# Row softmax, aligned code on DVE and ACT: padding that is executed instead of a branch over it

## The chip, the cores and the metric

One core of one Trainium2 chip. The time is that of one execution on the device in microseconds (us), the median of several. A profile of one execution goes with each kernel; its span runs from the first to the last instruction and is about 2 us shorter than the time (315.6 us of 317.42 in the kernel before). Engines: DVE is VectorE, ACT is ScalarE, SP is SyncE, which here only issues loads; "DVEq", "ACTq" and "SPq" are their sequencers.

## The reference

```python
def setup_inputs():
    batch, seq, dim = 32, 512, 1024
    return {
        "x": np.random.randn(batch, seq, dim).astype(np.float32),
        "temperature": 0.5,
    }

def reference(x, temperature):
    scaled = x / temperature
    shifted = scaled - np.max(scaled, axis=-1, keepdims=True)
    exp_x = np.exp(shifted)
    return (exp_x / np.sum(exp_x, axis=-1, keepdims=True)).astype(np.float32)
```

64 MiB are read and 64 MiB are written, 134 MB in all.

## The kernel before

Sixteen tiles of 128 partitions with eight rows each (4 MiB) go through six buffers. SP issues the loads; DVE takes the maximum of four rows per partition at a time and later multiplies by the reciprocal of the sum; ACT computes the exponential with its sum and issues the stores. A new load is issued when the store of the tile six places earlier has given its buffer free.

```python
TILES = [[8]] * 16
BUFS = 6
GROUP = 4
# ... cut: pools, groups, DRAM access patterns
    def load():                                   # on SP
        i = len(tiles)
        if i < len(TILES):
            xt = data.tile([P, sum(TILES[i]), d], f32, name="xt")
            nc.sync.dma_start(out=xt, in_=dram(xf, i))
            tiles.append(xt)
    # ... cut: maximum (DVE), exponential (ACT), divide (DVE)
    def store(g):                                 # on ACT, then the next load
        i, _, _, part = groups[g]
        if part:
            a, k = part
            nc.scalar.dma_start(out=dram(of, i)[:, a : a + k, :], in_=tiles[i][:, a : a + k, :])
            if a + k == sum(TILES[i]):
                load()

    with tc.manual_schedule():

        nc.vector.addr_align(128, offset=0, max_nops=0)
        nc.scalar.addr_align(128, offset=0, max_nops=0)
        for _ in range(BUFS):
            load()
        for g in range(len(groups) + 1):
            if g < len(groups):
                maximum(g)
                exponential(g)
            if g > 0:
                divide(g - 1)
                store(g - 1)
```

`addr_align(128, offset=0)` makes the next instruction of that engine lie at a multiple of 128 instruction slots. The slots up to there hold padding, of which the kernel's text doesn't tell the number. With `max_nops=0` a branch jumps over it (one COMPARE_BRANCH on each engine in the trace of the kernel before, 47 ns on DVE and 33 ns on ACT); with the default it is executed as NOPs.

Of the kernel before, what the change touches and what calls it, by code (L numbers as in the profile page):

```python
# [1 line left out]

# [4 lines left out]
# [9 lines that stand above are left out]
@with_exitstack  # L16
def kernel(
    ctx: ExitStack,
    tc: tile.TileContext,
    x: bass.AP,  # L20
    temperature: bass.AP,
    out: bass.AP,
):
    nc = tc.nc
    f32 = mybir.dt.float32
    scale = 1.0 / float(temperature)
    extreme = mybir.AluOpType.max if scale > 0 else mybir.AluOpType.min

    P = 128
    xf = x.flatten_outer_dims()  # L30
    of = out.flatten_outer_dims()
    n, d = xf.shape
    assert sum(sum(ks) for ks in TILES) * P == n

    data = ctx.enter_context(tc.tile_pool(name="data", bufs=BUFS))
    stats = ctx.enter_context(tc.tile_pool(name="stats", bufs=4))


    groups, first, r = [], [], 0
    for i, ks in enumerate(TILES):  # L40
        first.append(r)
        r += sum(ks)
        a = 0
        for k in ks:
            for b in range(0, k, GROUP):
                m = min(GROUP, k - b)
                groups.append((i, a + b, m, (a, k) if b + m == k else None))
            a += k

    def dram(t, i):  # L50
        k = sum(TILES[i])
        block = t[P * first[i] : P * (first[i] + k), :]
        return block.rearrange("(p k) d -> p k d", p=P, k=k)

    tiles, small = [], []

    def load():
# [6 lines that stand above are left out]
    def maximum(g):  # L64
        i, a, k, _ = groups[g]
        top, bias, sums, recip = (
            stats.tile([P, k], f32, name=name) for name in ("top", "bias", "sums", "recip")
        )
        small.append((bias, sums, recip))
        nc.vector.tensor_reduce(  # L70
            out=top, in_=tiles[i][:, a : a + k, :], axis=mybir.AxisListType.X, op=extreme
        )
        nc.vector.tensor_scalar_mul(bias, in0=top, scalar1=-scale)  # L73

    def exponential(g):
        i, a, k, _ = groups[g]
        bias, sums, _ = small[g]
        for b in range(k):
            nc.scalar.activation(  # L79
                tiles[i][:, a + b, :],  # L80
                tiles[i][:, a + b, :],
                mybir.ActivationFunctionType.Exp,
                bias=bias[:, b : b + 1],
                scale=scale,
                accum_out=sums[:, b : b + 1],
            )

    def divide(g):
        i, a, k, _ = groups[g]
        _, sums, recip = small[g]  # L90
        nc.vector.reciprocal(recip, sums)  # L91
        for b in range(k):
            nc.vector.tensor_scalar_mul(  # L93
                tiles[i][:, a + b, :], in0=tiles[i][:, a + b, :], scalar1=recip[:, b : b + 1]
            )

    def store(g):
# [8 lines that stand above are left out]

    with tc.manual_schedule():

        nc.vector.addr_align(128, offset=0, max_nops=0)
        nc.scalar.addr_align(128, offset=0, max_nops=0)  # L110
        for _ in range(BUFS):
            load()
        for g in range(len(groups) + 1):
# [8 lines that stand above are left out]
# [1 line left out]
_INS = ['x', 'temperature']  # L123
_OUTS = [((32, 512, 1024), 'float32')]

_NUMBERS = {'temperature': 0.5}


# [26 lines left out]
```

## Time and profile before

| | before |
|---|---|
| median time, 3 runs ahead of the prediction | 317.71 us (317.61 to 318.15) |
| span of the profiled run | 315.6 us |
| DVE busy, ACT busy | 75%, 47% |
| share of the DMA engines' time in loads and stores | 49.7% + 49.2% |
| first reduction on DVE | 13.42 us |

The chain of waits of its first 20 us (columns: start in us, length in us, what; the work that ended last, followed backwards) says what the first reduction waits for:

```profile
0.67 0.07 issue
0.73 12.66 DMA xt<-in_x_dram
13.39 0.02 issue
13.42 4.43 DVE top L70
```

The chain runs through SP's issue of the first load at 0.73 us and the load itself. The branches of DVE and ACT, taken at 0.8 and 0.7 us, aren't in it.

### The profile page before, as it was taken

Reading aid. Unit: us, or ns where it says so; the run is one execution under the profiler, and the core shown is the slowest. Engines: PE = TensorE matmul, PEld = TensorE weight load, DVE = VectorE, ACT = ScalarE, POOL = GpSimd, SP = SyncE. Lnnn points to the kernel's source line nnn. Section 1 sums busy time; section 2 is a strip of 40 time slices with the busy share of each in tenths; the row PEclk is TensorE's granted clock in tenths of the full one; section 3 lists DMA queues with packets and bytes.
Section 4 is the critical chain, followed back from the end, with each engine's and each line's share of the span. In section 5 each row is a group of like instructions: output and inputs, shape, how many; then the busy total and the mean of one; then the engine's idle time right before and its main releaser. Section 6 shows DMA issues by size and latency. Waiting matters only on the chain.

```text
span 315.6 us, 622 instructions
## 1 busy us (share of the span) xinstructions
DVE 235.5 (75%) x224; ACT 149.6 (47%) x257; POOL 0.2 (0%) x4
## 2 busy tenths in 40 slices
DVE  0299999999789494994939949498594976949720
ACT  0176666666626255361553615546065560645500
POOL 0000000000000000000000000000000000000000
DMA  8999999999999999999999999999999999999996
GB/s 330 415 448 415 386 457 407 461 411 453 424 440 432 432 432 429 444 424 453 415 454 407 457 407 457 403 461 403 461 403 461 403 462 403 461 419 444 428 436 278
DMA packets 4613, 134.26 MB, mean 425 GB/s; under 512 B 512, under 2 KB 512, under 8 KB 512
## 3 DMA queue, kind: packets, MB, share of 16 engines
q1 hardware_dynamic: 2304, 67.11, 49.7%
q10 hardware_dynamic: 2304, 67.11, 49.2%
q14 instruction: 5, 0.04, 0.0%
HBM read 67.11 MB, written 67.11 MB: 425 GB/s over the span
## 4 chain that ended last, share of the span: by engine, by line
DVE 72%; another core or an unknown queue 15%; DMA 4%; ACT 3%; issue 1%; DVEq 0%
DVE top L70 43%; DVE xt L93 27%; DMA xt<-in_x_dram 4%; ACT xt L79 3%; DVE recip L91 1%; DVE bias L73 1%; DVEq L150 0%
## 5 line engine op out<-in xcount | busy, mean ns | idle before, releaser
L79 ACT ACTIVATE xt<-xt,bias 128x1024 f32<-128x1024 f32 x128 | 145.4, 1137 | 136.0 <-DVE recip L91 118.6
L70 DVE TENSOR_REDUCE top<-xt 128x4 f32<-128x4096 f32 x32 | 141.3, 4416 | 62.2 <-DMA xt<-in_x_dram 62.2
L93 DVE TENSOR_SCALAR xt<-xt,recip 128x1024 f32<-128x1024 f32 x128 | 87.7, 749 | 1.1
L79 ACT ACTIVATION_READ_ACCUMULATOR xt<-xt,bias 128x1 f32 x128 | 23.8, 186 | 0.0
L79 ACT ACT_TABLE_LOAD x1 | 1.3, 1283 | 13.5 <-DMA xt<-in_x_dram 13.5
L91 DVE RECIPROCAL recip<-sums 128x4 f32<-128x4 f32 x32 | 5.5, 171 | 2.1 <-ACT xt L79 2.1
L73 DVE TENSOR_SCALAR bias<-top 128x4 f32<-128x4 f32 x32 | 5.5, 170 | 1.1
L136 POOL MEMSET const-bfloat16-1.0<- 128x1 bf16 x1 | 0.1, 102 | 0.0
L136 POOL MEMSET const-uint8-127<- 128x1 uint8 x1 | 0.1, 102 | 0.0
L136 POOL MEMSET const-float32-0.0<- 128x1 f32 x1 | 0.1, 99 | 0.2 <-issue 0.2
L136 POOL MEMSET const-float32-1.0<- 128x1 f32 x1 | 0.1, 99 | 0.0
## 6 DMA issues: line engine op xcount, KB each, us to landing
xt<-in_x_dram SPq DMA_DIRECT2D x16, 4096.0 KB, 50.2
out_dram<-xt ACTq DMA_DIRECT2D x16, 4096.0 KB, 38.4
```

Source lines behind the costliest of these rows:

```text
L70: nc.vector.tensor_reduce(out=top, in_=tiles[i][:, a : a + k, :], axis=mybir.AxisListType.X, op=extreme)
L73: nc.vector.tensor_scalar_mul(bias, in0=top, scalar1=-scale)
L79: nc.scalar.activation(tiles[i][:, a + b, :], tiles[i][:, a + b, :], mybir.ActivationFunctionType.Exp, bias=bias[:, b : b + 1], scale=scal ...
L91: nc.vector.reciprocal(recip, sums)
L93: nc.vector.tensor_scalar_mul(tiles[i][:, a + b, :], in0=tiles[i][:, a + b, :], scalar1=recip[:, b : b + 1])
L136: nc = _bacc.Bacc("TRN2", target_bir_lowering=False, num_devices=1)
```

## The change

The intent: the aligned code is to be reached by falling through the padding, not by a taken branch.

```diff
     with tc.manual_schedule():
 
-        nc.vector.addr_align(128, offset=0, max_nops=0)
-        nc.scalar.addr_align(128, offset=0, max_nops=0)
+        nc.vector.addr_align(128, offset=0)
+        nc.scalar.addr_align(128, offset=0)
         for _ in range(BUFS):
             load()
```

## The prediction

> **What bounds the kernel now.** The kernel is a row softmax over 64 MiB in and 64 MiB out on one core. I read the page first, and there the parts on DMA, because a softmax of this size does little arithmetic per byte.

> ```profile
> span 315.6 us, 622 instructions
> DVE 235.5 (75%) x224; ACT 149.6 (47%) x257; POOL 0.2 (0%) x4
> ...
> DMA  8999999999999999999999999999999999999996
> GB/s 330 415 448 415 386 457 407 461 411 453 424 440 432 432 432 429 444 424 453 415 454 407 457 407 457 403 461 403 461 403 461 403 462 403 461 419 444 428 436 278
> ...
> q1 hardware_dynamic: 2304, 67.11, 49.7%
> q10 hardware_dynamic: 2304, 67.11, 49.2%
> q14 instruction: 5, 0.04, 0.0%
> ```

> The reader is to see that the load queue q1 and the store queue q10 together fill 49.7 + 49.2 = 98.9% of the time of the 16 DMA engines, and that the DMA row is at 9 from the second slice to the last but one. No compute engine is near that: DVE is at 75%, ACT at 47%. 134.26 MB over 315.6 us are 425 GB/s. The line q14 is the fetch of instructions, five packets of about 0.04 MB / 5 = 8 KB each, nothing beside the rest.

> Next, the table by stretches (columns: length, busy us of DVE, ACT, POOL, clock, DMA share, GB/s). I cut it at the first DVE instruction, at the first long wait of DVE, in between, and at the issue of the last store.

> ```profile
> 0.00:13.40 13.40, 0.00 (x0) 0.00 (x0) 0.20 (x4) 1.00 0.89 361
> 13.40:85.00 71.60, 70.55 (x65) 45.86 (x78) 0.00 (x0) 1.00 1.01 430
> 85.00:160.00 75.00, 57.99 (x55) 35.98 (x63) 0.00 (x0) 1.00 1.00 433
> 160.00:235.00 75.00, 55.85 (x52) 35.26 (x62) 0.00 (x0) 1.00 1.00 433
> 235.00:302.00 67.00, 51.10 (x54) 32.46 (x56) 0.00 (x0) 1.00 1.00 431
> 302.00:315.60 13.60, 0.00 (x0) 0.00 (x0) 0.00 (x0) 1.00 0.82 354
> ```

> DMA is full in every stretch between the ends. DVE and ACT do nothing at all in the first 13.40 us and nothing in the last 13.60 us. The change touches only what these two do before their first work, so the first row is the one that matters. The timeline of the first 14 us, and what the branch lines show there (count, duration min/median/max, first and last start), say what happens in it:

> ```profile
> 0.73 2.89 SPq L61 DMA_DIRECT2D xt<-in_x_dram  x6
> 13.42 4.42 DVE L70 TENSOR_REDUCE top<-xt 128x4 f32<-128x4096 f32 x1 [13.42 <-DMA xt<-in_x_dram]
> 13.47 1.28 ACT L79 ACT_TABLE_LOAD   x1 [13.47 <-DMA xt<-in_x_dram]
> ```
> ```profile
> L109 DVEq COMPARE_BRANCH  x1: 47/47/47, 0.8 to 0.8; - x1
> ...
> L110 ACTq COMPARE_BRANCH  x1: 33/33/33, 0.7 to 0.7; - x1
> ```

> Lines 109 and 110 are the two alignment directives. In the kernel before each shows up as one branch, taken at 0.8 us (DVE) and 0.7 us (ACT), 47 and 33 ns long. Then both engines wait until the first 4 MB load lands at 13.4 us. Between the branch on DVE and the first reduction lie 13.42 - 0.85 = 12.57 us in which DVE has nothing to do.

> [...] the bare semaphore instructions of line 150 take 17 ns on ACT and 21 ns on DVE. [...]

> **The change part by part.** With the limit of zero the alignment is made by a branch over dead padding; without it the padding is executed. The instruction that follows lands at the same multiple of 128 slots in both kernels. The order of instructions per engine is the same in both, row for row (131 rows on DVE, 36 on ACT, 3 on SP), so nothing else moves.

> Removed: one branch per engine, 47 ns on DVE and 33 ns on ACT.

> Added: at most 127 padding instructions per engine[...]. That there is a branch on each engine shows that it is over zero on each. At the 21 ns of a bare sequencer instruction on DVE: 127 x 21 = 2.67 us at most, about 1.3 us for an average padding of 64. On ACT: 127 x 17 = 2.16 us at most, 1.1 us on average. So DVE would come to its first wait at 0.8 + 2.67 = 3.5 us at the latest, and ACT at 0.7 + 2.16 = 2.9 us. DVE's wait ends with the load at 13.4 us, so at least 9.9 us of slack are left on DVE, and more on ACT: its first activation starts at 18.08 us, once DVE's bias is there. What lies on the path that sets the end: 0. The load that ends the wait is issued by SP at 0.73 us, and SP has no alignment and no new instruction.

> Moved: fetches. [...] Each fetch packet is 8 KB of 134 MB[...]. [...] Sum for the end: 0.0 us. For the span and for the time outside it (317.4 us of the profiled run against a span of 315.6) I see no cause of change either, as both alignments come after the barrier at the program's start.

> **The rivals.**

> First, the padding is dear and reaches past the load. To delay DVE at all, 127 instructions would have to take 12.57 us, 99 ns each, nearly five times the 21 ns. [...] Against it speaks the 17 and 21 ns of the simple instructions. If it happened all the same, say at 150 ns each, DVE would start 6.5 us late. That would not be 6.5 us at the end: six loads of 4 MB are in the queue from the first 3.6 us, so DMA stays busy, and from 85 us on DVE waits again and again for loads. These are the rows that show its slack there:

> ```profile
> DVE top L70 <- DMA xt<-in_x_dram: 62.2, 12, 13.4
> DVE recip L91 <- ACT xt L79: 2.1, 2, 1.9
> ```

> 62.2 us in 12 waits, less the first of 13.4, leave 48.8 us in 11 waits, 4.4 us each. I would put such a case at 0 to 4 us more, 318 to 322 us: still within 2% (324.1).

> Second, the branch was costly and its removal gains. [...] the program would start sooner without it. Against: whatever DVE and ACT waited for a fetch ended before 13.4 us, as the first reduction starts at 13.42 us, 0.03 us after the load's landing, which the chain of waits puts at 0.73 + 12.66 = 13.39 us. A gain before that point is worth nothing. The time stays at 317.7 us.

> Third, the alignment shifts what follows after all, [...] so that fetches come at other points of the loop. The trace shows three fetches after the start, in the windows of 124 to 128, 160 to 164 and 252 to 256 us. Near none of them does DVE or ACT show an idle time that isn't put down to a load or to the other engine[...]. The time would stay within 0.3%.

> Fourth, chance in how loads and stores interleave. The rates per slice alternate between 403 and 461 GB/s, so a small shift at the start could settle in another pattern. The three runs before lie within 317.61 to 318.15 us, 0.17% of each other, which is the size I give it; the start of DVE is tied to the first load's landing in both kernels, so there is no shift to begin with.

> **Range and chances.** The centre is the median before, 317.7 us, with no term added: minus 0 for the branch, plus 0 for the padding. The spread of the runs before is 0.54 us; I take about 0.7 us below and 0.8 us above, for a new load of the program and for a part of the first rival: 317.0 to 318.5. A change of 2% is 6.4 us. Slower by that much would need more than the dear rival makes even when none of it is absorbed (6.5 us at 150 ns each), so 1%. Faster by that much would need a shorter DMA phase, with the same bytes, the same queues and DMA at 98.9%: 1%. Within 2%: 98%.

> **What would show each step right or wrong.** The two branch rows of lines 109 and 110 should be gone, or be replaced by padding instructions, if the profile lists them at all. The six load issues should still start at 0.73 us, the first reduction at 13.4 us with a wait put down to the load, the table load of ACT at 13.5 us. DVE's waits for loads should again add up to about 62 us in about 12 waits, the DMA row should stay at 9, and the two queues at about 49% each. Instruction packets may move in the first 4 us and should stay near 125, 162 and 253 us. I would be wrong if DVE's first reduction started later than 13.5 us, with a wait put down to issue and not to the load; then the padding costs over 99 ns per instruction or a fetch stalls for many microseconds. I would also be wrong if gaps without a named releaser appeared near the later fetches, or if the time moved by over 1 us with the first 14 us unchanged.

The sum for the end came to 0.0 us: nothing for the branch, and nothing for the padding (at most 2.67 us on DVE and 2.16 us on ACT, both inside the wait). The 17 and 21 ns are the lengths of bare semaphore instructions in the trace; that padding runs at that pace was the estimate.

## The result, and the profile after

The changed kernel took 317.87 us, median of 6 runs (317.49 to 317.99), against 317.60 us (317.43 to 318.15, 6 runs) for the kernel before. The ratio is 1.0004 with a 95% interval of 0.9991 to 1.0017: no change. Ratios here and below are the mean time of one kernel's fast runs over the mean of the other's fast runs of the same rounds, so not quite the ratio of the medians quoted beside them. Outputs agree with the reference.

From the page of the changed kernel:

```profile
span 315.7 us, 742 instructions
DVE 235.5 (75%) x224; ACT 149.6 (47%) x257; POOL 0.2 (0%) x4
...
DMA  8999999999999999999999999999999999999996
...
q1 hardware_dynamic: 2304, 67.11, 49.7%
q10 hardware_dynamic: 2304, 67.11, 49.2%
q14 instruction: 5, 0.04, 0.0%
```

742 instructions in place of 622: 120 more are 2 x 61 paddings less two branches. The other lines shown here are those of the kernel before, to the digit; the rates per slice (not shown) differ. The rows of the two alignment directives now read (count, duration in ns min/median/max, first and last start in us):

```profile
L109 DVEq NOP  x61: 18/18/18, 0.8 to 3.6; - x61
...
L110 ACTq NOP  x61: 14/14/14, 0.7 to 3.1; - x61
```

and the timeline of the first 14 us and the waits of DVE:

```profile
0.73 2.92 SPq L61 DMA_DIRECT2D xt<-in_x_dram  x6
13.61 4.42 DVE L70 TENSOR_REDUCE top<-xt 128x4 f32<-128x4096 f32 x1 [13.61 <-DMA xt<-in_x_dram]
13.66 1.28 ACT L79 ACT_TABLE_LOAD   x1 [13.66 <-DMA xt<-in_x_dram]
```
```profile
DVE top L70 <- DMA xt<-in_x_dram: 62.2, 12, 13.6
...
DVE recip L91 <- ACT xt L79: 2.1, 2, 1.9
```

Both engines are through with the padding by 3.6 and 3.1 us, and then still wait some 10 us for the first load, as before. The waits of DVE add up to the same 62.2 us in the same 12 waits. Two small things differ. The first reduction starts 0.19 us later, because the load landed later (12.86 us after its issue began, against 12.66). And instructions are fetched at other times: before, 8 KB packets of the instruction queue start at 1.8 and 3.6 us; after, both come at 7.3 to 7.4 us.

### The profile page after: what moved, and what is told of

It is laid out like the page before. It is cut to its first block, busy times and chain, and to the rows that moved or that the text cites. A ratio compares the mean times of both kernels' runs of the same rounds, so it can differ in the third digit from the quotient of the medians.

```text
span 315.7 us, 742 instructions
## 1 busy us (share of the span) xinstructions
DVE 235.5 (75%) x224; ACT 149.6 (47%) x257; POOL 0.2 (0%) x4
## 2 busy tenths in 40 slices
DMA  8999999999999999999999999999999999999996
DMA packets 4613, 134.26 MB, mean 425 GB/s; under 512 B 512, under 2 KB 512, under 8 KB 512
## 3 DMA queue, kind: packets, MB, share of 16 engines
q1 hardware_dynamic: 2304, 67.11, 49.7%
q10 hardware_dynamic: 2304, 67.11, 49.2%
HBM read 67.11 MB, written 67.11 MB: 425 GB/s over the span
## 4 chain that ended last, share of the span: by engine, by line
DVE 50%; DMA 27%; another core or an unknown queue 13%; ACT 4%; issue 1%; DVEq 0%; SPq 0%
DVE top L70 31%; DMA xt<-in_x_dram 20%; DVE xt L93 18%; DMA out_dram<-xt 8%; ACT xt L79 4%; DVE recip L91 1%; DVE bias L73 1%; DVEq L150 0%; SPq L61 0%
## 5 line engine op out<-in xcount | busy, mean ns | idle before, releaser
L79 ACT ACTIVATE xt<-xt,bias 128x1024 f32<-128x1024 f32 x128 | 145.4, 1137 | 135.8 <-DVE recip L91 118.5
L70 DVE TENSOR_REDUCE top<-xt 128x4 f32<-128x4096 f32 x32 | 141.3, 4416 | 62.2 <-DMA xt<-in_x_dram 62.2
L79 ACT ACTIVATION_READ_ACCUMULATOR xt<-xt,bias 128x1 f32 x128 | 23.8, 186 | 0.0
L79 ACT ACT_TABLE_LOAD x1 | 1.3, 1283 | 13.7 <-DMA xt<-in_x_dram 13.7
L91 DVE RECIPROCAL recip<-sums 128x4 f32<-128x4 f32 x32 | 5.5, 172 | 2.1 <-ACT xt L79 2.1
```

The lines of the kernel that those rows point to most:

```text
L70: nc.vector.tensor_reduce(out=top, in_=tiles[i][:, a : a + k, :], axis=mybir.AxisListType.X, op=extreme)
L79: nc.scalar.activation(tiles[i][:, a + b, :], tiles[i][:, a + b, :], mybir.ActivationFunctionType.Exp, bias=bias[:, b : b + 1], scale=scal ...
L91: nc.vector.reciprocal(recip, sums)
```

## The experiments

Twelve runs were made, one of them with the changed kernel itself. The first group asks whether the null result holds and what it rests on; then the same directive is moved to an engine without slack; then the slack of DVE is measured by filling it.

### The changed kernel again, and no alignment at all

First the changed kernel as it is, in five rounds.

> The changed kernel once more, beside the kernel before, in five rounds, as the measure of chance. Theory (the padding lies in DVE's and ACT's wait for the first load): ratio 1.000 within 0.002, 61 padding instructions on each of the two engines, the last one beginning near 3.6 us (DVE) and 3.1 us (ACT), and the first reduction within 0.3 us of 13.4 us, whichever way. Rival (the 0.19 us by which the first load landed later in the changed kernel's first profile is caused by the padding): the landing is again at 13.6 us and not at 13.4, and the time is 0.2 us above that of the kernel before.

Measured: 317.83 us against 317.79, ratio 1.0002 (0.9989 to 1.0014). The first reduction started at 13.72 us. So the first load landed late again, at 13.7 and not at 13.4 us, as the rival said of the landing. Its 0.2 us at the end don't show in the medians, but they can't be ruled out either: the interval reaches from 0.35 us less to 0.45 us more.

Then both directives are removed:

```diff
-        nc.vector.addr_align(128, offset=0, max_nops=0)
-        nc.scalar.addr_align(128, offset=0, max_nops=0)
```

> Both alignment directives are taken away, so neither branch nor padding is left and the code of DVE and ACT lies wherever it falls. Theory: ratio 1.000 within 0.002; the instruction packets come at other times than 123 to 125, 162 and 252 us, and nothing waits for them. Rival (where the code lies matters, and both kernels share a gain from the alignment): the time rises by 1 us or more and gaps without a named releaser appear at the fetches.

Measured: 317.88 us against 317.79, ratio 1.0001 (0.9988 to 1.0015). The code lies elsewhere: the fetches come at 65, 65, 182 and 240 us, none in the first 60 us, and the time is the same. In the timeline of this kernel the first load lands earliest of all:

```profile
12.91 4.42 DVE L70 TENSOR_REDUCE top<-xt 128x4 f32<-128x4096 f32 x1 [12.91 <-DMA xt<-in_x_dram]
```

12.91 us without any fetch in the first 13 us, 13.42 with fetches at 1.8 and 3.6, 13.61 and 13.72 with fetches at 7.3 to 7.5. DVE starts when the last of the 16 DMA engines that carry the load has landed its part: at 13.42 us after a last landing at 13.39 in the kernel before, at 13.61 after 13.59 in the changed kernel. Whether the fetches set these differences isn't shown: the median of the 16 is at 12.65 and 12.86 us, so the last is 0.7 us behind it in both kernels, and the 0.2 us between them aren't in the lag of one engine. The experiments with long padding below show such a lag at size. Neither the 0.5 us by which DVE starts earlier here than in the kernel before nor the 0.8 us against the run above shows at the end. That DVE's start isn't what sets it is tested further below.

### The same directive on SP, where there is no slack

SP's first load issue starts the chain, at 0.73 us. Four kernels add directives there; DVE and ACT stay as before. With one directive on SP:

```diff
+        nc.sync.addr_align(128, offset=0, max_nops=0)     # branch form
+        nc.sync.addr_align(128, offset=0)                 # padding form, in another kernel
```

and with two (again branch and padding form), so that more lies between:

```diff
+        nc.sync.addr_align(128, offset=0, max_nops=0)     # or without max_nops
+        nc.sync.addr_align(128, offset=127, max_nops=0)   # or without max_nops
```

A block is from here on a stretch of 128 slots that the directive aligns to. Every fetch packet within the spans of these traces is 8192 bytes. With 573 paddings (further below) the longer gaps between the paddings lie 128 slots apart; such a gap was 0.3 to 0.7 us in the runs with padding, 0.37 us on SP after its first 77.

Two directives, branch form:

> The kernel before, with two alignments in branch form on SP ahead of its first load issue, the second one 127 slots past the first, so that SP jumps over 127 to 254 dead slots. SP's issue sets the start of everything, so here the cost of a branch lies on the path that sets the end. Theory: two branch rows on SP of some 33 ns each, the first load issue 0.1 us later, the time up by 0.1 us[...]. Rival (nothing at the start counts, as loads run ahead): no change of time even if the first issue is later.

Two directives, padding form:

> As the run with branches on SP, but with padding: 127 to 254 padding instructions run on SP before the first load issue. At the 39 ns that ACT's padding took from one to the next in the changed kernel: 5.0 to 9.9 us. Theory: the first load issue moves from 0.73 us to 5.7 to 10.6 us, the first reduction moves with it, and the time rises by the same 5.0 to 9.9 us (1.6 to 3.1%). Rival (padding is free wherever it stands, because the DMA engines make up for a late start): the first issue is late but the time rises by less than half of that.

One directive, branch form:

> SP with one alignment in branch form, to a block's first slot, instead of two with the second to a block's last slot, which cost 2.1 us. Theory ([...] the 2.1 us came from landing on the last slot of a block [...]): the first load issue at 0.8 us lasts 0.4 us again and the time is within 0.3 us of the kernel before. Rival (any taken branch ahead of the first DMA issue costs a fetch): about 2 us again.

One directive, padding form:

> The run with one branch on SP, with padding instead: exactly the change of this study, on the engine that has no slack. The run with 204 paddings on SP had 127 of them from its second directive, so 77 are left here; at the 37 ns from one to the next seen there the first load issue comes at 0.73 + 77 x 0.037 = 3.6 us. Theory (on SP every late microsecond is paid, and the first issue after padding lasts 0.37 us as usual, against 2.34 us after the branch): time up by 2.5 to 3.0 us over the kernel before, so 0.3 to 0.9 us more than the 2.1 to 2.2 us of the branch. Rival (what cost 2 us behind the branch is the crossing into the new block, and padding crosses it too): first issue at 3.6 us and lasting 2.3 us, time up by 5 us.

| on SP | paddings run | first issue starts | it lasts | time | kernel before, same rounds | ratio (95%) |
|---|---|---|---|---|---|---|
| nothing (before) | 0 | 0.73 us | 0.37 us | | | |
| one branch | 0 | 1.16 | 2.34 | 319.80 us | 317.61 us | 1.0069 (1.0052 to 1.0086) |
| two branches | 0 | 1.35 | 2.32 | 319.92 | 317.79 | 1.0066 (1.0053 to 1.0078) |
| one padding | 77 | 3.98 | 2.17 | 322.26 | 317.62 | 1.0149 (1.0132 to 1.0166) |
| two paddings | 204 | 8.63 | 0.37 | 325.24 | 317.79 | 1.0234 (1.0220 to 1.0248) |

The rows of SP's own instructions carry it, first in the kernel before, then in these four (one branch; two branches; one padding; two paddings, where line 111 had run 77 and line 112 shows 127 more):

```profile
L61 SPq DMA_DIRECT2D xt<-in_x_dram x16: 327/328/517, 0.7 to 231.9; - x16
```
```profile
L61 SPq DMA_DIRECT2D xt<-in_x_dram x16: 327/328/2338, 1.2 to 233.5; - x16
```
```profile
L61 SPq DMA_DIRECT2D xt<-in_x_dram x16: 327/328/2318, 1.3 to 234.5; - x16
```
```profile
L111 SPq NOP  x77: 13/13/17, 0.7 to 3.6; - x77
...
L61 SPq DMA_DIRECT2D xt<-in_x_dram x16: 327/328/2172, 4.0 to 237.2; - x16
```
```profile
L112 SPq NOP  x127: 13/13/14, 3.9 to 8.6; - x127
...
L61 SPq DMA_DIRECT2D xt<-in_x_dram x16: 327/328/496, 8.6 to 240.0; - x16
```

The reader is to look at the maximum, the third of the durations (in the first and last row it belongs to a later issue). In three of the four kernels the first issue takes 2.2 to 2.3 us and not 0.37 us.

What follows. Padding is not free as such: on SP, 204 of them put the first issue 7.9 us later and cost 7.45 us (325.24 - 317.79). That settles the rival of the run with two paddings, that late starts are made up. The same run shows the pace in the end time, too: one padding followed the other after 37 ns; at 17 ns each, the length of a bare semaphore instruction on SP, 204 paddings would have cost 3.5 us. The branch costs far more than its 33 ns, about 2.2 us. The time lies inside the first issue (2.32 and 2.34 us in place of 0.37), and only 0.4 to 0.6 us ahead of it. My explanation for the run with two, landing on the last slot of a block, fell: the single branch lands on a first slot and costs the same. The rival in the run with one padding was right that padding pays as well when it runs into a new block and the first issue stands there. The sums agree: one branch makes the first issue 0.43 us later and 1.97 us longer, 2.40 us, of which 2.19 reach the end; one padding makes it 3.25 us later and 1.80 us longer, 5.05 us, of which 4.64 reach the end.

What the three slow issues have in common is that they are the kernel's first and that SP has just entered a block; 8 KB fetches start at 1.74 to 1.91 us in both branch kernels and at 4.6 us in the padded one, each while the first issue is on. With two paddings SP enters that block at 3.55 us, the fetch comes at 4.6 us under the padding, and the first issue at 8.63 us is of normal length. But a fetch that is due can't be the whole of it: in that same kernel the second issue, at 9.37 us, begins a new block too, whose fetch comes only at 13.98 us, and it lasts 0.33 us. What the first issue waits for stays open.

On the engine without slack the answer to the question of this study would have been the reverse of free: padding costs 4.6 us, the branch 2.2 us, and no directive nothing.

### Filling DVE's slack with padding

Four, six or eight whole blocks of padding are added to the 61 on both engines:

```diff
-        nc.vector.addr_align(128, offset=0, max_nops=0)
-        nc.scalar.addr_align(128, offset=0, max_nops=0)
+        nc.vector.addr_align(128, offset=0)
+        nc.scalar.addr_align(128, offset=0)
+        for engine in (nc.vector, nc.scalar):
+            for _ in range(4):          # 6, 8 in the other two
+                engine.addr_align(128, offset=127)
+                engine.addr_align(128, offset=0)
```

> 61 + 4 x 128 = 573 padding instructions on DVE and on ACT. At the 47 ns from one to the next that DVE showed: DVE reaches its first wait at 0.75 + 573 x 0.047 = 27.7 us, 14 us after the first load has landed. Theory (DMA is the bound; the engines' lateness costs nothing while the six loads that are queued keep DMA busy): these loads are 25.2 MB, at 430 GB/s done near 60 us when no store runs beside them, and the first store starts to move at 37 us in the kernel before, so some 23 us of lateness are free: the time rises by 0 to 1 us. Rival (only the 12.6 us until the first landing are slack, what goes beyond is paid one for one): the time rises by 14 us.

> 61 + 6 x 128 = 829 padding instructions on DVE and ACT: DVE reaches its first wait at 39.7 us, 26 us late. Theory: about at the edge of what the queued loads cover, the time rises by 1 to 5 us (26 less 23 is 3). Rival: it rises by 26 us.

> 61 + 8 x 128 = 1085 padding instructions on DVE and ACT: DVE reaches its first wait at 51.7 us, 38 us late. Theory: the queued loads are done near 60 us and the first store moves only near 75 us, so DMA stands still for some 15 us, which shows as empty slices, and the time rises by 12 to 18 us. Rival one (all lateness is paid): 38 us. Rival two (DMA catches up with any lateness): under 2 us.

| paddings per engine | first reduction | time | kernel before | ratio (95%) |
|---|---|---|---|---|
| 61 (the change) | 13.7 us | 317.83 us | 317.79 us | 1.0002 (0.9989 to 1.0014) |
| 573 | 29.5 | 324.40 | 317.71 | 1.0203 (1.0177 to 1.0229) |
| 829 | 42.5 | 325.68 | 317.71 | 1.0250 (1.0234 to 1.0265) |
| 1085 | 55.0 | 334.50 | 317.71 | 1.0528 (1.0510 to 1.0545) |

The longest wait of DVE with 573, 829 and 1085 paddings, "issue" standing for time with no wait that the profile names, which here is the padding:

```profile
DVE top L70 <- issue: 29.5, 1, 29.5
```
```profile
DVE top L70 <- issue: 42.5, 1, 42.5
```
```profile
DVE top L70 <- issue: 55.0, 1, 55.0
```

The DMA rows of the three pages, in 40 slices each (573, 829, 1085):

```profile
DMA  8999999999999999999999999999999999999980
```
```profile
DMA  8999999795999999999999999999999999999996
```
```profile
DMA  8999999309899999999999999999999999999997
```

In the third row DMA almost stands still in slices 8 and 9, near 60 to 75 us, as the theory of queued loads has it: the six loads are nearly done, and the first store packet starts at 75.6 us. The 16.8 us that the run lost (334.50 - 317.71) are in the 12 to 18 expected. The second row shows dips in slices 8 and 10; 8.0 us were lost where 1 to 5 were expected. The first row has no dip anywhere, and still 6.7 us were lost where 0 to 1 were expected. The rivals fail in all three: if all lateness were paid, 14, 26 and 38 us would have been lost, and with 1085 paddings under 2 us if all were made up. What the first row has is an end: a last slice at 0.

The trace notes for every transfer when each of the 16 DMA engines counts its part as landed (the tables below are worked out from the trace, in us, and are no view of the profile). For the last store:

```
                                       median of the 16   last of the 16   us behind
before                                      313.6              314.8          1.2
changed kernel                              313.7              314.9          1.2
573 paddings on DVE and ACT                 315.3              322.3          7.0
```

The median DMA engine finishes 1.7 us later than before; the last one is 7 us behind it. In the fifth load of the kernel with 573 paddings two of the 16 are far behind already (57.8 and 60.5 us, median 51.6), so the lag arises at the start. With 829 and 1085 paddings the landings of the last store lie together again, the last 1.0 and 0.8 us behind the median: there the loss is in the dips, not in the end. The next experiments take this apart.

### Lateness without fetches, fetches without padding, one engine alone

Three kernels. Late DVE by work:

```diff
+        idle = once.tile([P, 1024], f32, name="idle")      # a pool of its own, bufs=1
+        spare = once.tile([P, 1], f32, name="spare")
+        nc.vector.memset(idle, 0.0)
+        for _ in range(26):
+            nc.vector.tensor_reduce(out=spare, in_=idle, axis=mybir.AxisListType.X, op=extreme)
```

> The kernel before, with DVE made late by work instead of padding: a clear of a spare 128x1024 tile and 26 reductions of it, each about 1.1 us (a quarter of the 4.4 us of the 128x4096 one), so DVE reaches its first real reduction near 30 us, as with 573 padding instructions (29.5 us), but with 27 instructions and so without further instruction fetches. That run cost 6.7 us where 0 to 1 had been expected; in its trace two of the 16 DMA engines fell behind the other 14 by 9 us while the padding ran, and stayed behind. Theory (the fetches of the padding hold those two DMA engines up; lateness of DVE within 23 us is free): the time rises by 0 to 1 us and the landings of one transfer on the 16 engines stay within 3 us of each other. Rival (lateness itself costs, by another order of loads and stores): it rises by 5 to 8 us again.

The blocks of 573 paddings, jumped through:

```diff
+        for engine in (nc.vector, nc.scalar):
+            for _ in range(4):
+                engine.addr_align(128, offset=127, max_nops=0)
+                engine.addr_align(128, offset=0, max_nops=0)
```

> As the run with 573 padding instructions, but all in branch form: the same dead slots lie there, and DVE and ACT jump through them, two jumps per block of 128 slots, nine branches on each in all. The blocks still have to be fetched, but no padding runs. Theory (fetches are what cost): 13 or 14 instruction packets as with the padding, two DMA engines 5 us or more behind the others in the first loads, and the time up by 3 to 7 us although DVE starts within 1 us of 13.5 us. Rival (running the padding, or recording it, is what costs): the time within 1 us of the kernel before.

Long padding on ACT alone:

```diff
-        nc.vector.addr_align(128, offset=0, max_nops=0)
-        nc.scalar.addr_align(128, offset=0, max_nops=0)
+        nc.vector.addr_align(128, offset=0)
+        nc.scalar.addr_align(128, offset=0)
+        for engine in (nc.scalar,):
+            for _ in range(4):
+                engine.addr_align(128, offset=127)
+                engine.addr_align(128, offset=0)
```

> 573 padding instructions on ACT alone; DVE keeps its branch. ACT reaches its first wait at 25.4 us, so its first activation starts near 26.8 us, 8.7 us late, which the queued loads cover. Theory (each engine's fetches load one DMA engine): one of the 16 DMA engines falls behind by 5 to 9 us, the others stay together, and the time rises by 3 to 7 us. Rival (lateness of DVE is what cost 6.7 us): no more than 1 us.

One correction to what stands there: in the last of these DVE did not keep its branch but ran its 61 paddings, as in the changed kernel.

Measured, with 317.61 us for the kernel before:

| | first reduction | fetches in the first 35 us | time, fast runs |
|---|---|---|---|
| late by work | 35.0 us | 2 | 319.53 us (median of 4), ratio 1.0066 (1.0047 to 1.0086) |
| jumps | 23.5 | 10 | 321.79 and 322.57, ratio 1.0143 (1.0122 to 1.0165) |
| 573 paddings on ACT | 14.2 | 6 | 323.26, one run |

Two further runs of the jumps (328 and 340 us) and three of the padding on ACT (331 to 339 us) count as slow, being over 1.5% above the fastest run of the same kernel, and are left out. No other kernel shows such scatter, and the clock stands at 1.0 in all of these; its cause stays open. Over all four runs the medians are 325.44 and 334.86 us, so the losses given below for these two are the least that was seen; for the padding on ACT it is a single run.

The reductions took 1.25 us each from one to the next and not 1.1, so DVE was 21.6 us late (35.0 - 13.4), more than with 573 paddings (29.5 - 13.4 = 16.1), and lost 1.9 us, not 6.7. That is over the 0 to 1 us expected, at a lateness close to the 23 us where theory has the slack end, and far from the 5 to 8 us of the rival. The jumps run no padding but cost 4 to 5 us: with 13 instruction packets, against 14 with 573 paddings and 6 in the run late by work, the loss goes with the fetches and not with the paddings themselves or their records. DVE was late there as well, 10 us, which I hadn't expected: its jumps into a new block come 4.5 to 5.7 us apart. With ACT alone padded, DVE starts its first reduction 0.8 us late and ACT its first activation 8.8 us late (26.92 against 18.08 us), less than the 21.6 us of the run late by work, and 5.65 us are lost.

The stretches at the end, before and then late by work, 573 paddings, jumps and padding on ACT (columns: stretch, length, busy us of DVE, ACT, POOL with counts, clock, DMA share, GB/s):

```profile
310.00:315.00 5.00, 0.00 (x0) 0.00 (x0) 0.00 (x0) 1.00 0.53 229
315.00:320.00 5.00, 0.00 (x0) 0.00 (x0) 0.00 (x0) 1.00 0.00 0
```
```profile
310.00:315.00 5.00, 0.00 (x0) 0.00 (x0) 0.00 (x0) 1.00 0.87 374
315.00:320.00 5.00, 0.00 (x0) 0.00 (x0) 0.00 (x0) 1.00 0.03 13
```
```profile
315.00:320.00 5.00, 0.00 (x0) 0.00 (x0) 0.00 (x0) 1.00 0.12 52
320.00:325.00 5.00, 0.00 (x0) 0.00 (x0) 0.00 (x0) 1.00 0.02 7
```
```profile
310.00:315.00 5.00, 0.00 (x0) 0.00 (x0) 0.00 (x0) 1.00 0.58 249
315.00:320.00 5.00, 0.00 (x0) 0.00 (x0) 0.00 (x0) 1.00 0.08 33
```
```profile
310.00:315.00 5.00, 0.00 (x0) 0.00 (x0) 0.00 (x0) 1.00 0.56 242
315.00:320.00 5.00, 0.00 (x0) 0.00 (x0) 0.00 (x0) 1.00 0.06 26
```

A share of 0.06 is one of 16 DMA engines at work alone. The two engines of the 573 paddings make 0.12. Before, nothing of the kind follows the main part, and late by work next to nothing. The landings of the last store say how many are behind:

```
                               median   15th of 16   last     us behind (15th, last)
before                         313.6      314.8      314.8      1.2    1.2
late by work                   315.2      316.6      316.7      1.4    1.5
573 on DVE and ACT             315.3      319.7      322.3      4.4    7.0
jumps on DVE and ACT           313.9      318.8      320.0      4.9    6.1
573 on ACT alone               313.7      315.7      320.7      2.0    7.0
```

```
load                            1     2     3     4     5     6    first store packet starts at
late by work                  0.8   0.8   0.8   0.8   0.8   1.0    58.7
573 on ACT alone              1.4   2.8   3.3   3.3   6.8   7.3    45.6
jumps on DVE and ACT          2.3   4.3   5.2   5.3  10.1  10.1    47.2
573 on DVE and ACT            1.3   2.8   4.7   4.7   8.9   9.4    53.8
1085 on DVE and ACT           1.7   3.1   4.8   6.7   8.7   8.7    75.6
```

First the lag grows with the fetches: in the three middle kernels each engine with long padding or jumps has four more than in the run late by work, and at the fourth load 2.5 to 4.5 us more lag, so 0.6 to 1.1 us a fetch by this estimate, while a packet itself lasts 0.31 us (309 ns in each of the five of the changed kernel). Then it about doubles, from the fourth load to the fifth, though no fetch comes between 34 us and 125 us. By then stores run beside the loads (first store packet at 45.6 to 53.8 us); with 1085 paddings none runs before the sixth load is in, and there is no such step (6.7, 8.7 and 8.7 us from the fourth load to the sixth). Whether it is the stores that make the lag grow, no run shows by itself. Where the rest of the 0.6 to 1.1 us goes stays open.

A version that beats both kernels did not come out of this; the one without directives is as fast and simpler.

## Why the prediction was right or wrong

**Time: right, and not by luck.** 317.87 us against 317.7, in the range of 317.0 to 318.5, ratio 1.0004. The padding ran inside the wait for the first load, as the prediction had it; its one mis-sized cost (below) fell in that wait too.

**DMA is the bound, not DVE's start: shown.** Work that made DVE 21.6 us late cost 1.9 us, while 7.9 us of delay ahead of the first load issue cost 7.45. DMA had dips or stood still only when DVE was later than the queued loads cover (829 and 1085 paddings).

**Slack of 12.57 us at the start: right, and too narrow.** It counts only up to the first landing. A further 21.6 us of lateness cost 1.9 us, so what is nearly free goes on until the six queued loads are nearly done. The chain of waits passes through the first reduction all the same; being in that chain did not mean that a delay there was paid.

**Cost of the padding: mechanism right, term mis-sized.** The sum put "at most" 127 x 21 ns = 2.67 us on DVE and 2.16 us on ACT. There were 61 on each, and they took 2.86 us (0.75 to 3.61 us) and 2.39 us, over the stated maximum with half the count. The failing factor is the length of a bare semaphore instruction (21 and 17 ns), taken as the pace: one padding followed the other after 47 ns on DVE and 39 ns on ACT, 2.2 and 2.3 times as much. The row's own 18 and 14 ns are durations, not the distance from start to start. 127 would have taken 6.0 us, still inside.

**Branch of 47 and 33 ns: the record, not the cost.** On SP one branch of 33 ns cost 2.2 us. What the branches cost on DVE and ACT no run shows, as it lay in the wait; the second rival ("whatever DVE and ACT waited for a fetch ended before 13.4 us") describes it well.

**Fetches: moved as said, but not harmless in general.** The packets of the first 4 us moved to 7.3 us and the later ones stayed within 2 us of 125, 162 and 253. That they are "nothing beside the rest" held for five packets and fails for more: the volume is small, the lag of a single DMA engine is not (5.8 us more at the end with four more fetches). What an engine waits for a fetch was guessed; under full load, with a DMA share of 0.89 up to 13.4 us and 1.00 after, jumps into new blocks came 4.5 to 5.7 us apart on DVE and 1.9 to 5.8 us on ACT.

**First rival: the absorption was argued rightly, the fetches were left out.** For 6.5 us of lateness it named 0 to 4 us at the end. The run late by work fits that. With 573 paddings DVE was 16.1 us late and 6.7 us were lost, most of it in the lag of single DMA engines (5.8 us) that went with the fetches.

**Third and fourth rivals:** code placed elsewhere (no directive) gave 1.0001; the other pattern of rates per slice in the changed kernel went with no change of time. The fourth was wrong in that there would be no shift to begin with: the landing itself moved by 0.2 to 0.3 us.

**Signs.** The first reduction came at 13.61 and 13.72 us, past the 13.5 us that the prediction named as a sign of being wrong, but its wait was put down to the load and not to issue; the cause that the sign stood for wasn't there.

## What to carry to other kernels

Ask first what the engine would be doing at that moment: 61 paddings or one branch cost nothing above 0.2% before a 10 us wait, while the same directive ahead of the first DMA issue cost 2.2 us as a branch and 4.6 us as padding. A small DMA traffic is not judged by its bytes: in the one fast run with padding on ACT alone, four more fetches of 8 KB went with 5.65 us more time. The first load was done for DVE when the slowest of 16 engines was (median 12.65 us, last 13.39, DVE's start 13.42), so look at the last slices of the DMA row and at how far the landings of one transfer lie apart. And a chain of waits names what was waited for, not what a delay would cost; delay the thing on purpose and see.
